# Two-layer diffusion backbone: a fifth weight buffer, a new order at the three joins, spatial mixing inside its blocks, another pace for one gate

## The chip, the cores and the metric

The kernel runs on one core of a Trainium2 chip. The metric is the device time of one execution in microseconds (us). A core has a matrix engine (TensorE, PE in the profile; PEld is its weight load), a vector engine (VectorE, DVE), a scalar engine (ScalarE, ACT), GpSimd (POOL) and SyncE (SP, which here issues DMAs). Each engine takes its instructions from its own queue in a fixed order and waits on semaphores for the others. Matrix products and transposes write to PSUM; DVE and ACT bring the results back to SBUF.

## The reference

256 latent tokens and 256 context tokens of width 2048 go through two layers. What is computed, cut to what matters here:

```python
h, hc = x, ctx
for i in range(DEPTH):                                   # layer 0: attention, layer 1: gMLP
    sh1, sc1, g1, sh2, sc2, g2 = ada_params(c[:, None, :], ada_w[i], ada_b[i])
    a = h * (1 + sc1) + sh1
    y = na_mixer(...) if i % 2 == 0 else spatial_gating_mlp(a, *gm)
    h = layer_norm(ALPHA * h + g1 * y, ln_g[i, 0], ln_b[i, 0])
    f = swiglu(h * (1 + sc2) + sh2, ffn_w_in[i], ffn_w_out[i])
    h = layer_norm(ALPHA * h + g2 * f, ln_g[i, 1], ln_b[i, 1])

def spatial_gating_mlp(a, w_in, ln_g, ln_b, w_s, b_s, w_out):
    u, v = jnp.split(jax.nn.gelu(a @ w_in, approximate=False), 2, axis=-1)
    v = layer_norm(v, ln_g, ln_b).reshape(bsz, n // CHUNK, CHUNK, N_GROUPS, GROUP_DIM)
    v = jnp.einsum("gpq,bkqgc->bkpgc", w_s, v) + jnp.transpose(b_s)[:, :, None]
    return (u * v.reshape(bsz, n, D_MODEL)) @ w_out
```

`ada_params` is a product of SiLU(c) with a 2048 by 12288 matrix per layer. Everything is float32.

## The kernel before

**Products.** Each float32 operand is split into a high part (`S.copy` to float32r, line 91) and a low part (the difference, on DVE, line 92). Every product is three matmuls, lines 86 to 88: high by high, high by low, low by high. Weights arrive in pieces of 128x1024 (512 KB): `prefetch` (line 104) issues a piece's DMA on SP into one of `RAW` = 4 raw buffers and splits it into one of five pairs of hi and lo buffers (`hiA`, `hiB`); `piece` hands out one pair and keeps four more coming. Activations are split the same way by `act_split`, into `gh` and `gl`.

**Order.** The program is written in Python order, and a scheduler turns it into one fixed queue for each engine, ahead of the run. It goes by the order in the text, `tc.high_priority(n)` lets a part count as n places earlier, and `keep_in_program_order` (`pin`) pins an instruction to its place. It works from modelled durations; on the chip the queues hold whatever the real times are.

**Side work by ticks.** The adaLN vectors are computed beside the main work. Scales and shifts are dot products on DVE (line 150), and the gates are accumulated on DVE (`gate_task`, line 174: 32 products with 512 KB each) and then summed over the partitions by one `partition_all_reduce` on POOL (`sum_task`, line 189). These tasks are paced: `tick` (line 214) is called after about every piece, adds `rate` to a credit, or 0.3 of it when it also pops a task from `side`, and runs tasks while the credit covers their cost (0.5 each here). `pace(units)` sets the rate to the cost of all tasks over `units`, so they are spread over that many ticks. `need(...)` runs what is left of a gate or shift at once.

**Attention.** Heads come one after the other; a head's scores, softmax, transposes and values are the stages in `pend`, run by `advance`. After the last head the loop at line 603 empties `pend`. The output projection (`project_out` with `w_o`) is traced behind that.

**`project_out`** (line 718) makes a 256x2048 output from `kts` blocks of 128 and writes it in two column halves `nh` of two accumulators `n` for two token halves `b` (called half 0 and half 1 below). Behind each accumulator, `residual` (line 623) takes three DVE instructions: product with the gate, ALPHA times h plus that, and `bn_stats`. For the second column half, the last `HOLD` = 4 blocks are kept back, so that half 0 can be finished while half 1's products still run.

**The joins.** `finish(b, st)` then normalises token half b and starts the next input: `Modulated.first` takes the `moments` (bn_aggr, square root on ACT, reciprocal, offset: lines 632 to 638) and for two of four column quarters q calls `part` (line 677): normalise (DVE for even q, line 646; ACT for odd q, line 682), four transposes (line 688), scale and shift by four instructions of 128x128 (lines 694 and 696), and `split_into` of the whole 128x512 quarter. The next block's held products (`block_T` with `held`) start with half 0, go on with half 1, and `rest` makes the other quarters. There are three such joins: attention's output into the FFN of layer 0 (`f0`), that FFN into the gMLP (`m1`), the gMLP's output into the FFN of layer 1 (`f1`).

**gMLP.** Four blocks make v (`gv`), each eight pieces, then four blocks make u (`gu`). The layer norm's affine part on v is a list of eight side tasks (`av`), like that of h (`a1`) before it. `spatial(nb, g2)` (line 896) mixes two groups of block nb: for each group a matmul with `ws` into PSUM (line 904) and `u = (o + bs) * u` on DVE (line 905); both groups share a PSUM bank, and the second matmul waits for the first group's DVE instruction. Then four transposes (line 909) and a copy. Block nb - 1 is mixed behind block nb; the last block's mixing goes into `side`.

Of the kernel before, what the change touches and what calls it, by code (L numbers as in the profile page):

```python
# [39 lines left out]
HK0 = 3  # L40
RAW = 4
ADA = 6
# [5 lines left out]
EARLY = tuple((3 + 4 * g + h, h, 4 * g) for g in range(3) for h in range(4))  # L48
EN = 4
EARLY_END = {HK0 + h: 12 for h in range(4)}  # L50


@with_exitstack
def hybrid_kernel(ctx: ExitStack, tc: tile.TileContext, i, out):
# [220 lines left out]
    with tc.tile_pool(name="attnX", bufs=1) as px, ExitStack() as late:  # L275
# [208 lines left out]
        def t_tile(name):  # L484
            return mp.tile([P, 512], F32, tag="t", name=name, bufs=2)

        add_tasks(0, SH2, SC2, G1)
        pace(126)
        pend = []
        with tc.tile_pool(name="attnB", bufs=1) as pb:  # L490
# [104 lines left out]
            for h in range(NH):  # L595
                if h >= HK0:
                    proj_k(h)
                proj_q(h)
                if h in V_AT_Q:
                    while len(pend) > 8:  # L600
                        advance()
                    proj_v(V_AT_Q[h])
            while pend:
                advance()

    need((0, SH2), (0, SC2))
# [37 lines left out]
    def normalise(t3, b, nb, rs):  # L644
        sl = slice(nb * 512, (nb + 1) * 512)
        V.tensor_scalar(t3[:, b, sl], t3[:, b, sl], rs[:, 0:1], rs[:, 1:2], ALU.mult, ALU.add)

# [18 lines left out]
    class Modulated:  # L666
        def __init__(self, ln, layer, tsh, tsc, name):
            self.name = name
            self.ca = main.tile([P, KT], F32, tag="ca", name=f"ca{name}", bufs=2)
            self.cb = main.tile([P, KT], F32, tag="cb", name=f"cb{name}", bufs=2)  # L670
            V.tensor_tensor(self.ca, lncol[:, ln, 0, :], cols[:, layer, tsc, :], ALU.mult)
            V.tensor_tensor(self.cb, lncol[:, ln, 1, :], cols[:, layer, tsc, :], ALU.mult)
            V.tensor_tensor(self.cb, self.cb, cols[:, layer, tsh, :], ALU.add)
            self.xh = self.xl = None
            self.rs = {}

        def part(self, b, q):
            name, ca, cb = self.name, self.ca, self.cb
            tb = slice(b * P, (b + 1) * P)
            if q % 2:  # L680
                sl = slice(q * 512, (q + 1) * 512)
                S.activation(h_t[:, b, sl], h_t[:, b, sl], AF.Identity, bias=self.rs[b][:, 1:2], scale=self.rs[b][:, 0:1])
            else:
                normalise(h_t, b, q, self.rs[b])
            ps = t_tile(f"zt{name}{b}{q}")
            for j in range(4):
                kt = 4 * q + j
                T.transpose(ps[:, j * P : (j + 1) * P], h_t[:, b, kt * P : (kt + 1) * P], ident)
            tmp = main.tile([P, 4, P], F32, tag="zt", name=f"zs{name}{b}{q}", bufs=2)
            for j in range(4):  # L690
                kt = 4 * q + j
# [3 lines left out]
                else:  # L695
                    V.tensor_scalar(tmp[:, j, :], src, ca[:, kt : kt + 1], cb[:, kt : kt + 1], ALU.mult, ALU.add)
            ks = slice(4 * q, 4 * q + 4)
            split_into(self.xh[:, ks, tb], self.xl[:, ks, tb], tmp)

        def first(self, b, st):  # L700
# [3 lines left out]
            for q in range(2):  # L704
                self.part(b, q)

        def rest(self):
# [9 lines left out]

    def project_out(kts, src, key, name, finish, extra, last=False):
        st = stats_tile(name)
        hold = LAST if last else HOLD  # L720
        for nh in range(2):
            if nh == 0:
                ps = [[acc_tile(f"po{name}{nh}{n}{b}") for b in range(2)] for n in range(2)]
# [18 lines left out]

            k0 = 0
            if nh == 1:
# [6 lines left out]
                k0 = START  # L751
            k1 = kts - hold if nh == 1 else kts
            for kt in range(k0, k1):
                if nh == 1 and kt == max(k1 - 9, k0):
                    pos["extra"] = extra()
                w = piece() if nh == 0 or kt < k1 - START else take(1)[0]
# [4 lines left out]
                if nh == 0 or kt < k1 - QUIET:  # L761
                    tick()
# [6 lines left out]
            else:  # L769
                xs, ws = fetch(k1, hold)  # L770
                for b in range(2):
                    for n in range(2):
                        for j in range(hold):
                            products(k1 + j, xs[j], ws[j], n, b)
                        with tc.high_priority(AHEAD):
                            residual(ps[n][b], b, 2 + n, g, st, name)
                    if not last:
                        with tc.high_priority(AHEAD):
                            finish(b, st)
                if last:  # L780
# [26 lines left out]

    def ffn(layer, m, key, name, finish, free, last=False):
        pg = [acc_tile(f"pg{layer}{b}") for b in range(2)]
        block_T(m, pg, True)  # L810
        free.close()
        with tc.tile_pool(name=f"ffn{layer}", bufs=1) as pf:
# [30 lines left out]

            def extra():
                return outer.tile([P, 4, 1024], F32R, tag="xT", name=f"extra{layer}")

# [8 lines left out]
        KT, lambda k: oT[:, k, :], (0, G1), "wo", m.first,  # L855
        lambda: pw.tile([P, 4, 1024], F32R, tag="w", name="extra_o"),
    )
    affine_tasks(h_t, i["ln_row"][0], "a0")
# [4 lines left out]

    def begin(b, st):
        if b == 0:
            need((1, SH1), (1, SC1), (1, SH2), (1, SC2))
            m2.append(Modulated(1, 1, SH1, SC1, "m1"))
        m2[0].first(b, st)

    ffn(0, m, (0, G2), "d0", begin, free)  # L870


    m = m2[0]
    affine_tasks(h_t, i["ln_row"][1], "a1")
    add_tasks(1, G1)
    pace(62)
    free = ExitStack()
# [17 lines left out]

    def spatial(nb, g2):
        u = us[nb]
        tp = t_tile(f"uvt{nb}{g2}")
        sp = s_tile(f"sp{nb}{g2}")
        for j in range(2):  # L900
            g = nb * 4 + g2 * 2 + j
            c = slice((g2 * 2 + j) * P, (g2 * 2 + j + 1) * P)
            o = sp[:, j * NT : (j + 1) * NT].rearrange("p (b c) -> p b c", b=2)
            T.matmul(o, ws[:, g, :], vv[:, :, g * P : (g + 1) * P], start=True, stop=True)
            V.scalar_tensor_tensor(u[:, :, c], o, bs[:, g : g + 1], u[:, :, c], ALU.add, ALU.mult)
        for j in range(2):
            c = slice((g2 * 2 + j) * P, (g2 * 2 + j + 1) * P)
            for b in range(2):
                T.transpose(tp[:, j * NT + b * P : j * NT + (b + 1) * P], u[:, b, c], ident)
        S.copy(uT[:, nb * 4 + g2 * 2 : nb * 4 + g2 * 2 + 2, :], tp)  # L910

    for nb in range(NB):
        ps = [acc_tile(f"gu{nb}{b}") for b in range(2)]
        if nb == 0:
            rs = [moments(b, st, "v")[1] for b in range(2)]
            affine_tasks(vv, i["gm_row"], "av", rs)
        block_T(m, ps, False)
        us[nb] = pg.tile([P, 2, 512], F32, tag="u", name=f"u{nb}", bufs=2)
        for b in range(2):
            S.activation(us[nb][:, b, :], ps[b], AF.Gelu)  # L920
        if nb:
            for g2 in range(2):
# [140 lines left out]
```

## Time and profile before

| what | value |
|---|---|
| median of three runs | 2418.88 us (2416.48 to 2419.06) |
| the profiled execution | 2419.84 us |
| its span, first to last instruction | 2418.1 us |
| mean granted clock of TensorE in the span | 0.996 |
| DVE / ACT / POOL busy | 73% / 46% / 5% of the span |
| HBM read over the span | 606.46 MB, 252 GB/s |

How to read it: a row of the timeline gives the start and the duration in us, the engine, the line of the code, the operation, and the output and inputs by their tile names (buffer numbers left out). In brackets stands how long the engine was idle before it and what ended that. Lines 86 to 92 belong to helpers that every stage uses, so the tile names tell the stage: `powo`, `pod` and `pogo` are output projections, `pg` and `pu` FFN blocks, `gv` and `gu` gMLP blocks, `zt` and `zs` the transposes and scaled blocks at a join, `sp` and `uvt` the spatial mixing, `lw...` the low part of a weight piece, `gl...` that of an activation block. Matmuls overlap, so a PE row of 0.39 us starts every 0.227 us.

### The profile page before, as it was taken

How to read it: one execution, taken by the hardware profiler on the slowest of the kernel's cores; microseconds unless marked ns; L12 is line 12 of the kernel's file. 1: busy time of each engine (PE TensorE's matmuls, PEld its weight loads, DVE VectorE, ACT ScalarE, POOL GpSimd, SP SyncE). 2: the span in 40 equal slices, each digit the busy share in tenths (PEclk: the TensorE clock that was granted, in tenths of full speed). 3: DMA queues.
4: the chain of work that ended last, by engine and by line, in shares of the span. 5: the costliest groups of instructions: out<-in, count | busy, mean ns of one | idle time of the engine just before them, and what ended most of it. 6: DMA issues, size and time to landing. Idle time of an engine off the chain costs nothing. (4 is left out here: it accounts for less than half of the span.)

```text
span 2418.1 us, 31362 instructions
## 1 busy us (share of the span) xinstructions
PE 2381.7 (98%) x11624; PEld 1977.0 (82%) x11624; DVE 1755.7 (73%) x2155; ACT 1122.7 (46%) x1536; POOL 109.8 (5%) x55
## 2 busy tenths in 40 slices
PE   9999999999999999999999999999999999999998
PEld 6788988888788888888888788777888888888886
DVE  4877867677788877777889788787755555576666
ACT  4344534345644444444445554446544444445553
POOL 0000000020010200000000011020100000020000
PEclk9999999999999999999999999999999999999999
DMA  9977877756679899999989677756766677656563
GB/s 382 346 265 239 272 240 238 244 164 209 197 267 338 302 334 318 320 319 320 329 287 321 202 247 270 271 177 200 235 228 228 226 233 225 207 186 195 176 212 132
DMA packets 167827, 610.64 MB, mean 253 GB/s; under 512 B 19349, under 2 KB 21717, under 8 KB 163317
## 3 DMA queue, kind: packets, MB, share of 16 engines
q1 hardware_dynamic: 121172, 440.74, 54.3%
q10 hardware_dynamic: 46372, 167.86, 20.1%
q8 instruction: 91, 1.49, 0.3%
q14 instruction: 64, 0.52, 0.1%
q0 software_dynamic: 128, 0.03, 0.0%
HBM read 606.46 MB, written 2.10 MB: 252 GB/s over the span
## 5 line engine op out<-in xcount | busy, mean ns | idle before, releaser
L92 DVE TENSOR_TENSOR lwf<-rwf,hwf 128x1024 fp32r<-128x1024 f32 x320 | 407.2, 1275 | 278.9 <-ACT hwf L91 278.6
L91 ACT CAST hwf<-rwf 128x1024 fp32r<-128x1024 f32 x320 | 337.1, 1054 | 490.5 <-PE pu L88 221.6
L86 PE MATMUL pod<-hwd,ghd 128*128 128x512 f32 x684 | 266.4, 390 | 0.0
L87 PE MATMUL pod<-lwd,ghd 128*128 128x512 f32 x684 | 266.2, 389 | 0.0
L88 PE MATMUL pod<-hwd,gld 128*128 128x512 f32 x684 | 265.8, 389 | 0.0
L92 DVE TENSOR_TENSOR lwd<-rwd,hwd 128x1024 fp32r<-128x1024 f32 x172 | 212.2, 1235 | 64.0 <-ACT hwd L91 63.8
L150 DVE SCALAR_TENSOR_TENSOR ad<-ad,c_bc 128x1024 f32<-128x1024 f32 x192 | 232.6, 1219 | 0.6 <-DMA ad<-in_ada_t 0.6
L91 ACT CAST hwd<-rwd 128x1024 fp32r<-128x1024 f32 x172 | 180.6, 1050 | 54.8 <-PE pod L88 28.8
L174 DVE SCALAR_TENSOR_TENSOR gate<-ag,c_col,gate 128x1024 f32<-128x1024 f32 x128 | 163.2, 1282 | 0.0
L88 PEld LDWEIGHTS pod<-hwd,gld 128*128 128x128 f32 x684 | 128.3, 188 | 26.8
L86 PEld LDWEIGHTS pod<-hwd,ghd 128*128 128x128 f32 x684 | 128.4, 188 | 26.7 <-DVE sg L838 0.3
L87 PEld LDWEIGHTS pod<-lwd,ghd 128*128 128x128 f32 x684 | 128.4, 188 | 26.6
L86 PE MATMUL pg<-hwf,f1h 128*128 128x512 f32 x320 | 126.4, 395 | 0.0
L86 PE MATMUL pg<-hwf,f0h 128*128 128x512 f32 x320 | 126.4, 395 | 0.0
L87 PE MATMUL pg<-lwf,f0h 128*128 128x512 f32 x320 | 124.6, 389 | 0.4 <-DVE lwf L92 0.4
L88 PE MATMUL pg<-hwf,f1l 128*128 128x512 f32 x320 | 124.7, 390 | 0.0
L88 PE MATMUL pg<-hwf,f0l 128*128 128x512 f32 x320 | 124.7, 390 | 0.0
L86 PE MATMUL pu<-hwf,f0h 128*128 128x512 f32 x320 | 124.5, 389 | 0.0
L87 PE MATMUL pu<-lwf,f0h 128*128 128x512 f32 x320 | 124.5, 389 | 0.0
L88 PE MATMUL pu<-hwf,f0l 128*128 128x512 f32 x320 | 124.5, 389 | 0.0
L86 PE MATMUL pu<-hwf,f1h 128*128 128x512 f32 x320 | 124.5, 389 | 0.0
L87 PE MATMUL pu<-lwf,f1h 128*128 128x512 f32 x320 | 124.5, 389 | 0.0
(343 smaller groups left out, 5338.5 us busy)
## 6 DMA issues: line engine op xcount, KB each, us to landing
rwf<-in_w_in_t SPq DMA_DIRECT2D x320, 512.0 KB
ad<-in_ada_t ACTq DMA_DIRECT2D x192, 512.0 KB
rwd<-in_w_out SPq DMA_DIRECT2D x176, 512.0 KB
ag<-in_ada_g ACTq DMA_DIRECT2D x128, 512.0 KB
rwg<-in_w_gin SPq DMA_DIRECT2D x64, 512.0 KB
ap<-in_ada_p SPq DMA_DIRECT2D x20, 1024.0 KB
rwq<-in_w_q SPq DMA_DIRECT2D x32, 512.0 KB
rwo<-in_w_o SPq DMA_DIRECT2D x32, 512.0 KB
```

Of the source, the lines that this page charges most:

```text
L86: keep(T.matmul(ps, sh, mh, start=first, stop=False))
L87: keep(T.matmul(ps, sh, ml, start=False, stop=False))
L88: keep(T.matmul(ps, sl, mh, start=False, stop=last))
L91: S.copy(hi, src)
L92: V.tensor_tensor(lo, src, hi.bitcast(F32), ALU.subtract)
L150: pin(V.scalar_tensor_tensor(r, r, 1.0, c_bc[:, half * 1024 : (half + 1) * 1024], ALU.mult, ALU.mult, accum_out=o[:, nt : nt + 1],))
L174: pin(V.scalar_tensor_tensor(g, loaded.pop(key), c_col[:, kt, 0:1], g, ALU.mult, ALU.add))
```

## The change

It does seven things. There are five raw weight buffers in place of four. The first steps of attention's output projection are traced inside the loop that empties `pend`: two behind the last head's scores, one behind its transposes (`out_begin`, `WHILE`). At a join, half 1's residuals are queued behind half 0's first normalisation on DVE (`issue_after`). In `part`, for q = 0, the split is made two blocks at a time. The scales of the second join (`Modulated` m1) are made earlier, with the extra buffer. The gate of layer 1's mixer is paced over 44 units in place of 62. And `spatial` is cut into four steps, two `mix` and two `turn`, that `block_T` runs behind the third to sixth piece of the next block (the last block's four go into `side`).

```diff
-RAW = 4
+RAW = 5
+WHILE = {3: 2, 1: 1}
+        def out_begin(kts, src, name):
+            ps = [[acc_tile(f"po{name}0{n}{b}") for b in range(2)] for n in range(2)]
+
+            def step(kt):
+                w = piece()
+                x = act_split(src(kt), f"{name}0_{kt}")
+                for n in range(2):
+                    c = slice(n * 512, (n + 1) * 512)
+                    for b in range(2):
+                        tb = slice(b * P, (b + 1) * P)
+                        mm3(ps[n][b], x[0][:, tb], x[1][:, tb], w[0][:, c], w[1][:, c], kt == 0, kt == kts - 1)
+                tick()
+
+            return ps, step
...
+            wo_ps, wo_step = out_begin(KT, lambda k: oT[:, k, :], "wo")
+            wo_k = 0
             while pend:
                 advance()
+                for _ in range(WHILE.get(len(pend), 0)):
+                    wo_step(wo_k)
+                    wo_k += 1
...
-                normalise(h_t, b, q, self.rs[b])
+                ins = normalise(h_t, b, q, self.rs[b])
+                self.mark = self.mark or ins.ins
...
+            cut = 2 if q == 0 else 4
...
-            ks = slice(4 * q, 4 * q + 4)
-            split_into(self.xh[:, ks, tb], self.xl[:, ks, tb], tmp)
+                if (j + 1) % cut == 0:
+                    ks = slice(kt + 1 - cut, kt + 1)
+                    split_into(self.xh[:, ks, tb], self.xl[:, ks, tb], tmp[:, j + 1 - cut : j + 1, :])
...
+                m = None
                 for b in range(2):
                     for n in range(2):
                         for j in range(hold):
                             products(k1 + j, xs[j], ws[j], n, b)
-                        with tc.high_priority(AHEAD):
+                        with tc.high_priority(AHEAD), tc.issue_after(m.mark) if m else nullcontext():
                             residual(ps[n][b], b, 2 + n, g, st, name)
                     if not last:
                         with tc.high_priority(AHEAD):
-                            finish(b, st)
+                            m = finish(b, st)
...
-    def begin(b, st):
-        if b == 0:
-            need((1, SH1), (1, SC1), (1, SH2), (1, SC2))
-            m2.append(Modulated(1, 1, SH1, SC1, "m1"))
-        m2[0].first(b, st)
+    def prepare():
+        need((1, SH1), (1, SC1), (1, SH2), (1, SC2))
+        m2.append(Modulated(1, 1, SH1, SC1, "m1"))
...
-    pace(62)
+    pace(44)
...
+        def mix(g2):
+            sp = s_tile(f"sp{nb}{g2}")
+            for j in range(2):
...
+                T.matmul(o, ws[:, g, :], vv[:, :, g * P : (g + 1) * P], start=True, stop=True)
+                V.scalar_tensor_tensor(u[:, :, c], o, bs[:, g : g + 1], u[:, :, c], ALU.add, ALU.mult)
+
+        def turn(g2):
+            tp = t_tile(f"uvt{nb}{g2}")
...
+            S.copy(uT[:, nb * 4 + g2 * 2 : nb * 4 + g2 * 2 + 2, :], tp)
+
+        return [partial(f, g2) for f in (mix, turn) for g2 in range(2)]
...
-        block_T(m, ps, False)
+        block_T(m, ps, False, spatial(nb - 1) if nb else ())
...
-        if nb:
-            for g2 in range(2):
-                spatial(nb - 1, g2)
-    side.extend((lambda: spatial(NB - 1, 0), lambda: spatial(NB - 1, 1)))
+    side.extend(spatial(NB - 1))
```

More of the change, by code (lines that the diff above doesn't have):

```diff
@@ L1 @@
-from contextlib import ExitStack
+from contextlib import ExitStack, nullcontext
 from functools import partial
@@ L645, in normalise @@
         sl = slice(nb * 512, (nb + 1) * 512)
-        V.tensor_scalar(t3[:, b, sl], t3[:, b, sl], rs[:, 0:1], rs[:, 1:2], ALU.mult, ALU.add)
+        return V.tensor_scalar(t3[:, b, sl], t3[:, b, sl], rs[:, 0:1], rs[:, 1:2], ALU.mult, ALU.add)
     def affine_tasks(t3, src, name, rs=None):
@@ L675, in __init__ @@
             self.rs = {}
+            self.mark = None
         def part(self, b, q):
@@ L705, in first @@
                 self.part(b, q)
+            return self
         def rest(self):
@@ L716, in hybrid_kernel, with project_out @@
     AHEAD = 400
-    def project_out(kts, src, key, name, finish, extra, last=False):
+    def project_out(kts, src, key, name, finish, extra, last=False, begun=None):
         st = stats_tile(name)
@@ L722, in project_out @@
             if nh == 0:
-                ps = [[acc_tile(f"po{name}{nh}{n}{b}") for b in range(2)] for n in range(2)]
+                ps, step, k0 = begun or (*out_begin(kts, src, name), 0)
+                for kt in range(k0, kts):
+                    step(kt)
             else:
@@ L741, in fetch @@
                 return xs, take(n)
-            k0 = 0
             if nh == 1:
@@ L751, in project_out @@
                 k0 = START
-            k1 = kts - hold if nh == 1 else kts
-            for kt in range(k0, k1):
-                if nh == 1 and kt == max(k1 - 9, k0):
+            k1 = kts - hold
+            for kt in range(k0, k1) if nh == 1 else ():
+                if kt == max(k1 - 9, k0):
                     pos["extra"] = extra()
-                w = piece() if nh == 0 or kt < k1 - START else take(1)[0]
+                w = piece() if kt < k1 - START else take(1)[0]
                 x = act_split(src(kt), f"{name}{nh}_{kt}")
@@ L760, in project_out @@
                         products(kt, x, w, n, b)
-                if nh == 0 or kt < k1 - QUIET:
+                if kt < k1 - QUIET:
                     tick()
@@ L806, in block_T, with ffn @@
                 turn.pop(0)()
-    def ffn(layer, m, key, name, finish, free, last=False):
+    def ffn(layer, m, key, name, finish, free, last=False, prepare=None):
         pg = [acc_tile(f"pg{layer}{b}") for b in range(2)]
@@ L844, in extra @@
             def extra():
+                if prepare:
+                    prepare()
                 return outer.tile([P, 4, 1024], F32R, tag="xT", name=f"extra{layer}")
@@ L856, in hybrid_kernel @@
         lambda: pw.tile([P, 4, 1024], F32R, tag="w", name="extra_o"),
+        begun=(wo_ps, wo_step, wo_k),
     )
@@ L862, in hybrid_kernel @@
     m2 = []
-    def begin(b, st):
-        if b == 0:
-            need((1, SH1), (1, SC1), (1, SH2), (1, SC2))
-            m2.append(Modulated(1, 1, SH1, SC1, "m1"))
-        m2[0].first(b, st)
-    ffn(0, m, (0, G2), "d0", begin, free)
+    def prepare():
+        need((1, SH1), (1, SC1), (1, SH2), (1, SC2))
+        m2.append(Modulated(1, 1, SH1, SC1, "m1"))
+    ffn(0, m, (0, G2), "d0", lambda b, st: m2[0].first(b, st), free, prepare=prepare)
     m = m2[0]
@@ L894, in hybrid_kernel, with spatial @@
     us = {}
-    def spatial(nb, g2):
+    def spatial(nb):
         u = us[nb]
[L898 to L910, printed above, removed]
+        def mix(g2):
+            sp = s_tile(f"sp{nb}{g2}")
+            for j in range(2):
+                g = nb * 4 + g2 * 2 + j
+                c = slice((g2 * 2 + j) * P, (g2 * 2 + j + 1) * P)
+                o = sp[:, j * NT : (j + 1) * NT].rearrange("p (b c) -> p b c", b=2)
+                T.matmul(o, ws[:, g, :], vv[:, :, g * P : (g + 1) * P], start=True, stop=True)
+                V.scalar_tensor_tensor(u[:, :, c], o, bs[:, g : g + 1], u[:, :, c], ALU.add, ALU.mult)
+        def turn(g2):
+            tp = t_tile(f"uvt{nb}{g2}")
+            for j in range(2):
+                c = slice((g2 * 2 + j) * P, (g2 * 2 + j + 1) * P)
+                for b in range(2):
+                    T.transpose(tp[:, j * NT + b * P : j * NT + (b + 1) * P], u[:, b, c], ident)
+            S.copy(uT[:, nb * 4 + g2 * 2 : nb * 4 + g2 * 2 + 2, :], tp)
+        return [partial(f, g2) for f in (mix, turn) for g2 in range(2)]
     for nb in range(NB):
```

## The prediction

> **What bounds the kernel now.** First the page's head, to see which engine fills the span. Then the waits of PE (total us, times, longest).
>
> ```profile
> span 2418.1 us, 31362 instructions
> PE 2381.7 (98%) x11624; PEld 1977.0 (82%) x11624; DVE 1755.7 (73%) x2155; ACT 1122.7 (46%) x1536; POOL 109.8 (5%) x55
> ...
> PE pt L575 <- ACT p L565: 3.7, 2, 3.4
> PE ztf L688 <- ACT zsf L694: 2.3, 2, 1.2
> PE pogo L88 <- DVE glgo L92: 2.3, 2, 1.3
> PE sp L904 <- DVE u L905: 2.1, 1, 2.1
> ...
> PE pg L86 <- ACT f0h L91: 1.8, 2, 1.6
> PE pg L86 <- ACT f1h L91: 1.8, 2, 1.6
> PE gv L86 <- ACT m1h L91: 1.8, 2, 1.6
> ...
> PE s L86 <- ACT qh L515: 0.3, 1, 0.3
> ```
>
> TensorE is busy for 98%, and the change leaves all its products in place. So only its waits can be won: one inside attention (pt), two at each of the three joins (pg or gv, then zt), one in the first spatial mix (sp), two in the gMLP output (pogo). A wait costs more than its length where the clock drops. The windows view shows it (PE busy, clock, DMA share):
>
> ```profile
> 642.20:645.60 3.40, 1.62 (x7) 1.00 0.46 145
> 645.60:649.00 3.40, 3.40 (x9) 0.50 0.17 57
> 1382.87:1386.28 3.41, 2.10 (x8) 1.00 0.49 159
> 1522.80:1526.20 3.40, 3.34 (x11) 0.50 0.79 321
> 1673.00:1676.40 3.40, 3.40 (x10) 0.50 0.29 82
> ```
>
> Three stretches of 3.4 us ran at half clock, each behind a wait, and cost 1.7 us each. At the second join PE was busy for 2.10 of 3.41 us and the clock held; at the first, for 1.62 of 3.40, and it fell.
>
> The Trainium skill ("TensorE: Matmul & The Clock Gate", Part 1) throttles after a whole idle window of about 3.4 us. Here 1.8 idle us in 3.4 sufficed, so the rows decide; by the page alone the joins would have no half clock to lose, and the sum below would be 3.4 us higher.
>
> **The joins.** DVE and then ACT at the second join, from the timeline:
>
> ```profile
> 1378.70 0.67 DVE L626 TENSOR_TENSOR yd<-pod,gate 128x512 f32<-128x512 f32 x1
> 1379.29 0.15 DVE L638 SCALAR_TENSOR_TENSOR rsm<-mvm,rsm 128x1 f32<-128x1 f32 x1
> 1379.40 0.69 DVE L627 SCALAR_TENSOR_TENSOR h_t<-h_t,yd 128x512 f32<-128x512 f32 x1
> 1380.01 0.54 DVE L646 TENSOR_SCALAR h_t<-h_t,rsm 128x512 f32<-128x512 f32 x1
> ...
> 1379.26 1.06 ACT L91 CAST hwg<-rwg 128x1024 fp32r<-128x1024 f32 x1 [0.67 <-PE pod L88]
> 1380.21 1.52 ACT L682 ACTIVATE h_t<-h_t,rsm 128x512 f32<-128x512 f32 x2
> 1381.64 1.83 ACT L694 ACTIVATE zsm<-ztm,cbm,cam 128x128 f32<-128x128 f32 x5
> 1383.35 0.62 ACT L91 CAST m1h<-zsm 128x512 fp32r<-128x512 f32 x1
> ```
>
> Half 1's product (L626) and sum (L627) stand on either side of L638, which yields half 0's offset, and ahead of half 0's normalisation (L646). Issued behind it, they free 1.1 us on DVE (L646 from 1380.01 to about 1378.95). ACT's cast of the next weights at 1379.26 stays, so ACT's own normalisation (L682) doesn't move; the casts by twos do the rest. m1h waited for five L694 at 0.34 us; now it waits for two and casts half the columns: 1.0 us for the three, and 0.2 us for the cast (an estimate: the 128x256 casts of gh take 0.41 us). That is 1.2 us at least, 2.3 if all of DVE's lead counts, against 1.8 waited. I take 1.6 each, **-4.8** for three; the rest stays as a wait for m1l, which still queues on DVE behind a 1.2 us weight difference. The waits for zs at the transposes of half 1 fall by the same casts: **-1.5** of 2.8 (2.3 at the FFN joins, 0.5 at the second). Half clocks at two joins: **-3.4**.
>
> What is late next is half 1. Its chain starts at the end of PE's products, which hardly moves, while PE now comes 1.6 to 3.3 us sooner to its transposes:
>
> ```profile
> 1387.53 1.22 DVE L92 TENSOR_TENSOR extra<-rwg,extra 128x1024 fp32r<-128x1024 f32 x1
> 1388.66 0.54 DVE L646 TENSOR_SCALAR h_t<-h_t,rsm 128x512 f32<-128x512 f32 x1
> ...
> 650.21 1.00 DVE L646 TENSOR_SCALAR h_t<-h_t,rsf 128x512 f32<-128x512 f32 x2
> ...
> 652.08 1.03 PE L688 MATMUL ztf<-ident,h_t 128*128 128x128 f32 x8
> ```
>
> At the second join the last normalisation ends at 1389.20 and PE wanted it at 1389.36: no slack. At the first the earlier of two normalisations ended at 650.75 (0.54 behind 650.21), and PE came at 652.08: 1.3 us to spare. So new waits of about 0.9 us at the second join and 1.4 at each FFN join: **+3.7** (bounds 0, if the weight differences leave the chain, and 6). The joins together: **-6.0**, from -10 to 0. Half 1's first residual, queued behind the normalisation, is itself 0.5 us later; the second can't start before PE's last products, so nobody waits for that. Moving the column scales (`prepare`) ahead takes three DVE instructions of 0.16 us out of a place that isn't on this path: 0.
>
> **The sum of the gate, moved by pace 44.** The (1, G1) gate is 32 products at 0.5 and one partition sum at 0.5: 16.5 units. gv has 28 ticks and gu 32, of which the 16 with a side task count 0.3. At 62 the 32nd product fell into the gMLP output. At 44 it needs 16/0.375 = 42.7 counted ticks: after tick 36 there are 24.8, so tick 54, the second piece of gu's last block. The count can be checked: at 62 the 23rd product (11.5/0.266 = 43.2) belongs to tick 55, the third piece of that block, and there it is:
>
> ```profile
> 1557.30 1.23 DVE L92 TENSOR_TENSOR lwg<-rwg,hwg 128x1024 fp32r<-128x1024 f32 x1 [1.50 <-ACT hwg L91]
> 1558.44 1.28 DVE L174 SCALAR_TENSOR_TENSOR gate<-ag,c_col,gate 128x1024 f32<-128x1024 f32 x1
> ...
> 1558.24 0.39 PE L87 MATMUL gu<-lwg,m1h 128*128 128x512 f32 x1
> 1558.47 0.39 PE L88 MATMUL gu<-hwg,m1l 128*128 128x512 f32 x1
> ...
> 1605.01 12.78 POOL L189 PARTITION_ALL_REDUCE gate<-gate  x1 [101.88 <-DVE gate L174]
> 1606.02 9.30 DVE L92 TENSOR_TENSOR glgo<-uT,ghgo 128x256 fp32r<-128x256 f32 x1
> ...
> 530.59 8.84 DVE L92 TENSOR_TENSOR lwq<-rwq,hwq 128x1024 fp32r<-128x1024 f32 x1
> ```
>
> The partition sum on POOL starts right behind the last product, and the next difference of two SBUF operands on DVE, 0.42 us long elsewhere, hangs until 10.3 us after its start. Both big waits that aren't joins come from this: pt (530.59) and pogo (1606.02). At its new place the last product runs one piece (twelve matmuls 0.227 us apart, 2.72 us) before 1558.44, ends near 1557.0, and DVE is shut until 1567.3. The change puts the mixes of spatial(2) behind the third and fourth piece of that block, at 1558.5 and 1561.2, and each mix needs DVE between its two matmuls:
>
> ```profile
> 1522.33 0.87 DVE L905 SCALAR_TENSOR_TENSOR u<-sp,bs,u 128x256 f32<-128x256 f32 x2
> 1512.31 6.50 DMA rwg<-in_w_gin
> ```
>
> (There sp waited 2.1 us for L905 alone.) PE takes its queue in order, so everything behind the second matmul waits. If the weight difference of 1557.30, 0.3 us after the sum's start, still slips through, the first mix passes and the second holds PE from 1562 to 1568, 6.2 us; if not, the first does, from 1559.2 to 1568, 8.8 us. I take **+6.5**, nearer to the first, and one stretch of half clock, **+1.7**. In exchange the pogo waits go: **-2.3**.
>
> The Trainium skill ("SBUF — State Buffer", Who interferes with whom) has a DVE instruction with at most one SBUF input free of GpSimd. L905 reads PSUM and one SBUF tile, so by the page it would pass; but it queues behind differences with two.
>
> **The first mix, and the fifth buffer.** spatial(0) moves from behind its block into it, behind the third piece. That hides the mix under products, but nearer to the eight `av` tasks, which keep DVE full (the second row is DVE's alone: 29.3 of 30 us):
>
> ```profile
> 1450.00:1470.00 20.00, 20.00 (x90) 16.57 (x89) 17.19 (x16) 9.30 (x10) 0.00 (x0) 1.00 1.00 361
> ...
> 1480.00:1510.00 30.00, 29.30 (x36) 1.00 0.60 202
> ...
> 1505.46 0.39 PE L88 MATMUL gu<-hwg,m1l 128*128 128x512 f32 x1
> 1509.93 1.22 DVE L92 TENSOR_TENSOR lwg<-rwg,hwg 128x1024 fp32r<-128x1024 f32 x1
> ```
>
> PE ends the third piece at 1505.7; DVE is through with what comes ahead of the mix at about 1511. Some of these 5.5 us are in the planned order, so I take a wait of 1.6 us with its half clock, 3.3, against 2.1 + 1.7 now: **-0.5** (from -3.8 to +6.0, rival 3). The fifth raw buffer lets the piece issued at 1512.31 (6.50 us to land) start one release earlier. No PE wait but this one follows such a landing, so I give it 0 by itself (from -1 to 0.5, the length of the smaller waits); its 4 KB a partition take no engine's time. The gate's loads come denser too: 512 KB of weights and 0.75 of 512 KB in a tick of 2.72 us make 337 GB/s. From 1450 to 1470 DMA moved 361 GB/s, and PE was busy for all 20 us: hidden.
>
> **Attention's tail.** The three steps of the output projection ahead of the last transposes fill a place in which PE lists only the 0.3 us of s: the scheduler already puts this projection's products there. The pt wait lies a head earlier and stays. **-0.3** (0 to -0.8).
>
> **The sum**, against the profiled execution's own 2419.84 us (span 2418.1 and 1.7 around it): -6.0 - 2.3 + 6.5 + 1.7 - 0.5 - 0.3 = -0.9, so 2418.9. That run lies 0.96 above the median of the three, 2418.88; so **2418.0 us**, no change that can be measured. About 0.2%, 4.8 us, is what a measurement of this kernel can tell.
>
> **The rivals.**
> 1. *The sum misses the mixes.* If the last product runs two pieces earlier or later than counted, as products in pogo ran ahead of their ticks, DVE is shut between mixes. For it: DVE has no other reason to hold L174 back. Against it: four products of the last two gu blocks stand at the counted piece. +8.2 becomes about +0.5: **2410.3**. Chance 0.28.
> 2. *Half 1 isn't late.* If its normalisations move ahead of the weight differences, the 3.7 us go: **2414.3**. Nothing in the order of before says so. 0.10.
> 3. *Slower.* The gates come 1.4 times as often, so by the first mix DVE has done six products more; two of them (2.6 us) fall in the full stretch. Then L905 comes 8.1 us after PE asks, with 1.7 of half clock: 9.8 against 3.8 now, 6.5 more than taken: **2424.5**. It decides once DVE is over 7 us behind at the third piece of gu's second block. 0.20.
>
> **How the numbers follow.** The forecast has 0.42, with 2412 to 2424 as its own range (joins from -10 to 0, the hold from 6.2 to 8.8). Of it I count 0.07 as faster and 0.06 as slower; rival 1 gives 0.27, rival 2 0.06, rival 3 0.16. So faster 0.40, same 0.38, slower 0.22. The range that leaves 2 in 10 out is **2406 to 2426**.
>
> **What would show it.** A POOL sum starting near the second piece of gu's last block, a DVE difference of 9 us behind it, and a PE wait of 6 to 9 us on sp show the main step right; sums elsewhere, or mixes through before it, show it wrong. At the joins L646 should stand right behind L638, m1h should be cast in 128x256 pieces, and the first pg and gv waits be under 0.6 us; a longer wait of zt for L646 or L682 shows half 1 late. Half-clock stretches: one in gu's last block, none at the joins.

## The result, and the profile after

| | us | against before |
|---|---|---|
| before, median of 5 runs | 2418.88 (2416.48 to 2421.66) | |
| changed kernel, median of 5 runs | 2429.06 (2427.12 to 2429.58) | 1.0042, 95% interval 1.0027 to 1.0057 |
| its profiled execution | 2429.58, span 2427.5 | 9.74 above the profiled execution of before |

The change made the kernel slower by 0.42%, 10.2 us; 2418.0 was forecast. In the rows of the changed kernel L93 is the difference of a split (before: L92), L175 the gate's product (L174), L647 to L649 the residual (L626 to L628), L667 the normalisation on DVE (L646), L711 the transposes (L688), L934 and L935 the two halves of a spatial mix (L904, L905; L906 and L907 in the kernels that are the one before with the twos).

The page's head:

```profile
span 2427.5 us, 31382 instructions
PE 2381.7 (98%) x11624; PEld 1978.0 (81%) x11624; DVE 1757.8 (72%) x2161; ACT 1121.8 (46%) x1542; POOL 106.6 (4%) x55
```

PE is busy for the same 2381.7 us as before, so the loss is waiting and slowed products. PE's waits (total, times, longest):

```profile
PE sp L934 <- DVE u L935: 10.9, 2, 7.8
PE ztf L711 <- DVE h_t L667: 3.6, 4, 1.5
PE pt L591 <- ACT p L581: 3.4, 1, 3.4
...
PE ztm L711 <- DVE h_t L667: 1.8, 2, 1.5
...
PE gv L87 <- ACT m1h L92: 1.1, 1, 1.1
PE gv L89 <- DVE m1l L93: 0.9, 1, 0.9
```

The rows of pg for f0 and f1 are those of gv for m1 within 0.1. The wait for sp was 2.1 us and is 10.9. The transposes now wait for L667 some 1.8 us at each join, 1.5 of it (the longest) for half 1, where before they waited 0.2 for half 0 alone. The wait for a first cast is 1.1, not 1.6; the 1.1 is half 1's, though (the timeline has it behind half 1's transposes). The pogo waits (2.3) are gone. The stretches of half clock, each under the stretch ahead of it (PE busy, clock, DMA share, GB/s), from the windows view:

```profile
647.77:651.18 3.41, 1.71 (x11) 1.00 0.84 268
651.18:654.59 3.41, 3.41 (x10) 0.50 0.25 103
1385.05:1388.46 3.41, 1.61 (x11) 1.00 0.84 258
1388.46:1395.29 6.83, 5.99 (x17) 0.50 0.28 101
1511.30:1514.70 3.40, 0.68 (x3) 1.00 0.89 307
1514.75:1518.16 3.41, 3.41 (x9) 0.50 1.00 382
1562.53:1565.95 3.42, 0.04 (x1) 1.00 0.00 0
1565.95:1576.19 10.24, 5.82 (x14) 0.50 0.33 104
```

Two lie at joins, one behind spatial(0), one in gu's last block. Half of PE's busy time in them is lost: 1.7, 3.0, 1.7 and 2.9 us. (Attention's tail has a stretch of its own in every trace here, 3.41 us long in some and 6.83 in others, with the change or without, and so has the end.) What happened in that last block, from the timeline:

```profile
1558.34 1.28 DVE L175 SCALAR_TENSOR_TENSOR gate<-ag,c_col,gate 128x1024 f32<-128x1024 f32 x1
...
1559.72 11.88 POOL L190 PARTITION_ALL_REDUCE gate<-gate  x1 [54.63 <-DVE gate L175]
1559.83 10.09 DVE L93 TENSOR_TENSOR lwg<-rwg,hwg 128x1024 fp32r<-128x1024 f32 x1 [0.21 <-ACT hwg L92]
...
1561.27 0.60 PE L934 MATMUL sp<-vv,ws 128*128 128x256 f32 x2
...
1569.84 0.47 DVE L935 SCALAR_TENSOR_TENSOR u<-sp,bs,u 128x256 f32<-128x256 f32 x1
...
1570.37 1.22 PE L934 MATMUL sp<-vv,ws 128*128 128x256 f32 x2 [7.80 <-DVE u L935]
```

The last product of the gate ends, the partition sum starts, and the weight difference 0.11 us behind it takes 10.09 us. The first mix of spatial(2) begins on PE 1.55 us behind the sum's start; its part on DVE runs only at 1569.84, behind that difference, and PE's next product of the mix waited 7.80 us for it.

By stage, from the first and last products of each (the profiled executions, in order): start -2.8 us, attention's tail +0.2, first join -1.1, second join with gv +4.9, gu +15.1, gMLP output -5.9, third join with the last FFN -0.9. The start's -2.8 isn't the change's: its first query product comes at 153.4 to 154.1 in all the runs below, with four raw buffers too, and only the one profiled execution of before has 156.2. Some 2.6 us of gu's +15.1 and the output's -5.9 are spatial(2) itself, which moved from the one stage to the other.

### The profile page after: what moved, and what is told of

The parts are those of the page before. It is cut to its first block, busy times and chain, and to the rows that moved or that the text cites. A ratio compares the mean times of both kernels' runs of the same rounds, so it can differ in the third digit from the quotient of the medians.

```text
span 2427.5 us, 31382 instructions
## 1 busy us (share of the span) xinstructions
PE 2381.7 (98%) x11624; PEld 1978.0 (81%) x11624; DVE 1757.8 (72%) x2161; ACT 1121.8 (46%) x1542; POOL 106.6 (4%) x55
## 4 chain that ended last, share of the span: by engine, by line
PE 93%; DVE 4%; DMA 1%; issue 1%; ACT 1%; POOL 0%; DVEq 0%; SPq 0%; POOLq 0%; ACTq 0%
PE pu L87 7%; PE pu L88 7%; PE pu L89 7%; PE pod L88 6%; PE pod L89 6%; PE pod L87 6%; PE pg L87 6%; PE pg L89 6%; PE pg L88 6%; PE vps L87 2%; PE vps L88 2%; PE vps L89 2%; PE kps L88 2%; PE kps L89 2%; PE kps L87 2%; PE qps L89 1%
## 5 line engine op out<-in xcount | busy, mean ns | idle before, releaser
L93 DVE TENSOR_TENSOR lwf<-rwf,hwf 128x1024 fp32r<-128x1024 f32 x320 | 406.1, 1272 | 275.8 <-ACT hwf L92 275.8
L92 ACT CAST hwf<-rwf 128x1024 fp32r<-128x1024 f32 x320 | 336.8, 1053 | 484.2 <-PE pu L89 242.2
L93 DVE TENSOR_TENSOR lwd<-rwd,hwd 128x1024 fp32r<-128x1024 f32 x172 | 210.0, 1223 | 63.0 <-ACT hwd L92 62.7
L92 ACT CAST hwd<-rwd 128x1024 fp32r<-128x1024 f32 x172 | 180.3, 1048 | 55.3 <-PE pod L89 33.3
L175 DVE SCALAR_TENSOR_TENSOR gate<-ag,c_col,gate 128x1024 f32<-128x1024 f32 x128 | 163.7, 1286 | 0.0
L89 PE MATMUL pu<-hwf,f1l 128*128 128x512 f32 x320 | 124.5, 389 | 0.0
```

The source lines that it names most:

```text
L89: keep(T.matmul(ps, sl, mh, start=False, stop=last))
L92: S.copy(hi, src)
L93: V.tensor_tensor(lo, src, hi.bitcast(F32), ALU.subtract)
L175: pin(V.scalar_tensor_tensor(g, loaded.pop(key), c_col[:, kt, 0:1], g, ALU.mult, ALU.add))
```

## The experiments

Theory: the sum of the gate under the mixes of spatial(2) made the loss. Rivals: the joins made it; or the sum costs the same wherever it stands. Each ratio is to runs of before on the same chip (their medians were 2415.9 to 2417.6), with its 95% interval; 0.1% is 2.4 us.

| | what it is | ratio |
|---|---|---|
| e1 | changed kernel, pace 62 | 1.0026 (1.0015 to 1.0037) |
| e2 | changed kernel, pace 39.5 | 1.0021 (1.0012 to 1.0029) |
| e3 | changed kernel, no tie | 1.0023 (1.0014 to 1.0031) |
| e4 | changed kernel, no twos | 1.0051 (1.0038 to 1.0065) |
| e5 | no tie, pace 39.5, mixes two pieces later | 1.0006 (0.9997 to 1.0015) |
| e6 | no tie, pace 39.5 | 0.9987 (0.9978 to 0.9996) |
| e7 | before with the twos | 0.9983 (0.9974 to 0.9992) |
| e8 | before with the fifth buffer | 0.9982 (0.9973 to 0.9990) |
| e9 | before with twos and fifth buffer | 0.9970 (0.9958 to 0.9982) |
| e10 | e9 at pace 39.5 | 1.0019 (1.0010 to 1.0028) |
| e11 | no tie, pace 39.5, mixes behind blocks | 1.0018 (1.0009 to 1.0027) |
| e12 | changed kernel, mixes behind blocks | 0.9999 (0.9990 to 1.0008) |
| e13 | e9 at pace 44 | 0.9983 (0.9974 to 0.9992) |
| e14 | no tie, pace 62 | 1.0000 (0.9991 to 1.0010) |

### Where the sum stands (e1, e2, e12)

```diff
-    pace(44)
+    pace(62)      # e1
+    pace(39.5)    # e2
```

> The changed kernel, but the gate's products are spread at pace 62 as before the change, so that its partition sum goes back into the gMLP output. Theory A (the loss is the sum standing under the mixes of spatial(2)): the 7.98 us wait of sp and the half clock behind it go, some 11 us, and the pogo wait with its half clock comes back, some 4 us: about 2422 us (2419 to 2425), so no longer slower than before by more than 0.2%. Rival B (the loss comes from the joins, whose new waits and half clocks stay here): within 3 us of the changed kernel's 2429. Rival C (the sum costs the same wherever it stands): 2427 to 2430, with a PE wait of about 8 us in the gMLP output.

> The changed kernel with pace 39.5: by the count of ticks the 32nd product then belongs to the sixth piece of gu's third block, and the sum's 10 us of DVE lie between the mixes of spatial(1) and those of spatial(2). Theory A: the partition sum starts near that piece, one DVE difference behind it still takes 9 to 10 us, but PE waits for none of it: no sp wait over 2 us in the last block, no pogo wait: 2418 us (2415 to 2421), some 11 us under the changed kernel. Rival C (wherever the sum stands in gu, PE runs out of weights while DVE is shut): a PE wait of 5 us or more behind the long difference and 2424 or more. Rival B (the joins): 2427 to 2430.

Both came out in between: 0.16% and 0.21% below the changed kernel, not 0.3 to 0.45%. The 7.8 us wait went in both, as the theory had it. In e1 its place was taken by a wait in the gMLP output (PE's waits):

```profile
PE pogo L89 <- DVE glgo L93: 4.3, 2, 3.3
...
PE sp L934 <- DVE u L935: 2.8, 1, 2.8
```

142 of the output's products start ahead of the sum here, and 118 before: it came two pieces of twelve products later. (By the clock it stands 34.9 us behind the output's first product here, 1609.93 less 1575.05, and 32.0 before, 1605.01 less 1572.98; the 2.6 us of spatial(2) lay in that stretch before.) By the code, this is because the changed kernel's spatial(3) is cut into four side parts, not two, each of whose ticks counts 0.3. DVE's backlog then ran into the residual of the output's first half: in e14, which has the same two pogo waits, L647 to L649 fill DVE from 1624.00 to 1629.97, ahead of the split that PE wanted at 1627. In e2 the denser gates made the first mix worse:

```profile
PE sp L934 <- DVE u L935: 5.2, 2, 4.8
```

So the wait that the theory named went, and other costs came in its place; these two runs alone don't say what the sum's place is worth. e12 leaves the sum where the change puts it and takes the mixes away from it:

```diff
-        return [partial(f, g2) for f in (mix, turn) for g2 in range(2)]
+        return [partial(f, g2) for g2 in range(2) for f in (mix, turn)]
...
-        block_T(m, ps, False, spatial(nb - 1) if nb else ())
+        block_T(m, ps, False)
...
+        if nb:
+            for part in spatial(nb - 1):
+                part()
```

> The changed kernel with only the spatial mixes taken back behind their blocks: tie, twos, pace 44 and fifth buffer stay. Theory: the sum still starts at the second piece of gu's last block (about 1558 us) and one difference on DVE still takes 10 us, but spatial(2) comes behind the block, when DVE is free again, so the 8 us wait and its half clock (11 us) go, and the wait of spatial(0) falls from 3.4 to 1 to 2.5 us: 10 to 14 us less than the changed kernel, 2415 to 2419, within 0.2% of before. Rival: PE runs out of weights during the 10 us (a wait on lwg of 5 us or more in the last block), and the time stays over 2424.

It is 0.43%, 10.4 us, below the changed kernel, as expected. The sum still starts there, 3.3 us earlier by the clock, and DVE (timeline) still stands still:

```profile
1555.08 1.28 DVE L175 SCALAR_TENSOR_TENSOR gate<-ag,c_col,gate 128x1024 f32<-128x1024 f32 x1
1556.65 11.14 DVE L93 TENSOR_TENSOR lwg<-rwg,hwg 128x1024 fp32r<-128x1024 f32 x2 [0.30 <-ACT hwg L92]
1567.72 3.48 DVE L93 TENSOR_TENSOR lwgo<-rwgo,hwgo 128x1024 fp32r<-128x1024 f32 x3
...
1572.74 0.92 DVE L935 SCALAR_TENSOR_TENSOR u<-sp,bs,u 128x256 f32<-128x256 f32 x2
```

Two differences take 11.14 us where such a one takes 1.22 elsewhere, yet PE (windows: PE busy, clock, DMA share, GB/s) goes on:

```profile
1540.00:1590.00 50.00, 49.39 (x227) 1.00 0.49 162
```

The weights cast ahead carry PE through 10 us without DVE. What can't be carried is a mix, which needs DVE between two matmuls. That settles the theory against both rivals for this term: same joins, same pace, the same sum in the same block, and the 10 us are gone.

### The tie of half 1's residual, and the twos (e3, e4, e6, e7)

```diff
-                        with tc.high_priority(AHEAD), tc.issue_after(m.mark) if m else nullcontext():
+                        with tc.high_priority(AHEAD):      # e3
...
-            cut = 2 if q == 0 else 4
+            cut = 4                                        # e4
```

> The changed kernel, but the residual of half 1 isn't tied behind the normalisation of half 0 (only that tie is taken out; the casts by twos stay). The tie took the 0.67 and 0.69 us of half 1 out of half 0's way at three joins. If it is worth what the prediction gave it (two thirds of 1.6 us a join), the first PE waits (gv and pg for m1h, f0h, f1h) grow by about 1 us each and half 1's waits at the transposes (1.70 and 1.35) shrink by as much or less: 2429 to 2432. If half 1 is what decides the joins now, the first waits grow and half 1's shrink by the same, and the time stays within 1.5 us of 2429.

> The changed kernel, but the first blocks are cast whole again (four transposed blocks at a time). Half 0's first cast then comes some 1 us later at each join. If half 0 decides: the first waits for m1h, f0h and f1h go from 1.1 to about 2 us and half 1's waits fall: 2429 to 2432. If half 1 decides (PE comes too soon to its transposes in any case): within 1.5 us of 2429, or up to 3 us below it, since the three small casts and three differences that the twos add go off ACT and DVE ahead of half 1's normalisation.

Neither expectation for e3 was right: without the tie the kernel is 0.19% faster. The same pair at the other paces gives 0.34% (e2 less e6) and 0.26% (e1 less e14): some 5 to 8 us. e3's waits at the joins:

```profile
PE gv L87 <- ACT m1h L92: 1.3, 2, 0.6
...
PE gv L89 <- DVE m1l L93: 0.7, 1, 0.7
...
PE ztm L711 <- DVE h_t L667: 0.2, 1, 0.2
```

(pg's for f0 and f1 are the same within 0.1.) About 2.2 us a join, against 3.8 with the tie (1.8, 1.1 and 0.9). The tie does save half 0's first product its wait of 0.6; but half 1 pays 1.5 for L667 and 0.5 more for its own cast. DVE at the second join shows how. With the tie (changed kernel), from half 1's second residual to its normalisation:

```profile
1378.98 0.69 DVE L647 TENSOR_TENSOR yd<-pod,gate 128x512 f32<-128x512 f32 x1
...
1380.53 1.22 DVE L93 TENSOR_TENSOR lwg<-rwg,hwg 128x1024 fp32r<-128x1024 f32 x1
1381.66 0.68 DVE L649 BATCH_NORM_STATS2 std<-h_t 128x6 f32<-128x512 f32 x1
...
1382.86 0.25 DVE L653 BATCH_NORM_AGGREGATE mvm<-std 128x2 f32<-128x24 f32 x1
...
1385.37 1.22 DVE L93 TENSOR_TENSOR lwg<-rwg,hwg 128x1024 fp32r<-128x1024 f32 x1
1386.50 1.00 DVE L667 TENSOR_SCALAR h_t<-h_t,rsm 128x512 f32<-128x512 f32 x2
```

Without it (e3):

```profile
1376.50 1.21 DVE L93 TENSOR_TENSOR lwg<-rwg,hwg 128x1024 fp32r<-128x1024 f32 x1
...
1377.94 0.68 DVE L647 TENSOR_TENSOR yd<-pod,gate 128x512 f32<-128x512 f32 x1
...
1379.85 0.69 DVE L649 BATCH_NORM_STATS2 std<-h_t 128x6 f32<-128x512 f32 x1
...
1380.90 0.26 DVE L653 BATCH_NORM_AGGREGATE mvm<-std 128x2 f32<-128x24 f32 x1
...
1384.16 1.00 DVE L667 TENSOR_SCALAR h_t<-h_t,rsm 128x512 f32<-128x512 f32 x2
1385.08 1.22 DVE L93 TENSOR_TENSOR lwg<-rwg,hwg 128x1024 fp32r<-128x1024 f32 x1
```

L667 stands 7.52 us behind the second L647 with the tie and 6.22 without. The second residual starts at PE's last product either way. But half 1's first residual, put behind half 0's normalisation, takes the place in which DVE did a weight difference (1376.50); with the tie that difference falls into half 1's chain, ahead of L649, and another goes ahead of L667.

No trace of a kernel with the twos and without the tie has a half clock at a join (e3, e5, e6, e7, e9, e10, e11, e13, e14); each trace with the tie has at least one (changed kernel, e1, e2, e4, e12).

e4, the tie without the twos, is 0.09% above the changed kernel, inside what the runs can tell. Its waits for L667 are 5.3 us at the three joins as with the twos (5.4), its zs waits are back (3.8), and its waits for first casts are shorter (1.7 for 3.3): nearer to the second answer. The twos by themselves:

> The kernel before with the first blocks cast by twos, nothing else of the change. The prediction's -4.8 for the first waits came from DVE's order and the twos together. If the twos do it alone: the waits of 1.6 us for f0h, f1h and m1h fall to about 0.6 each, the zs waits go, and one or two half clocks with them: 4 to 6 us below before. If the tie is needed for it: first waits of 1.2 or more, and within 2 us of before.

0.17%, 4.1 us. The waits of e7 at the second join, and below them that of before for the low part:

```profile
PE gv L86 <- ACT m1h L91: 1.3, 2, 0.6
...
PE gv L88 <- DVE m1l L92: 0.7, 1, 0.7
```

```profile
PE gv L88 <- DVE m1l L92: 0.2, 1, 0.2
```

At each join the waits for a cast went from 1.8 to 1.3 (two of 0.6), but the wait for the low part rose by as much. What the twos won are the zs waits (2.8 us at the three joins) and the half clocks there; e7's 11 runs have a mean granted clock of 0.9968 and the 33 of before on that chip 0.9959, which puts some 2 us of the gain down to the clock. The tie isn't needed for it.

> The changed kernel without the tie and at pace 39.5; mixes where the change puts them. If the two gains are separate (tie some 5 us, sum some 8 us on the same chip), this is the changed kernel less 12 to 13 us: 2415 to 2418, within 0.2% of before, with an sp wait of 3 to 5 us left at spatial(0) and no other wait over 2 us behind the second join. If they overlap (half clocks shared), 2419 to 2421.

0.13% below before, 2415.8 us where before is 2418.9: the gains of pace and tie add up.

### The mixes inside the blocks (e5, e10, e11, e14), and the best version (e8, e9, e13)

```diff
-    def block_T(m, ps, held, turn=()):
+    def block_T(m, ps, held, turn=(), at=2):
...
-            if turn and k2 >= 2:
+            if turn and k2 >= at:
...
+        block_T(m, ps, False, spatial(nb - 1) if nb else (), 4)
```

> The changed kernel without the tie of half 1's residual, at pace 39.5, and with the four parts of a spatial mix behind the fifth to eighth piece of a block in place of the third to sixth. Theory: the first mix of spatial(0) waits because DVE is still behind with the av rows and the gate's products when PE asks behind the third piece; two pieces (5.4 us) later DVE has caught up. Then the sp waits (5.2 us at pace 39.5) fall under 1.5 us, the half clock of gu's second block goes, and with the tie gone the joins' 1.5 us waits of half 1 too: 0.2 to 0.5% below before, 2407 to 2414 us. Rival: DVE stays behind by as much (it is full as long as gates come at this pace), the wait is 4 us again two pieces later, and the time is that of e6.

The theory failed: two pieces later costs 0.19% against e6, and the first mix still waits 3.9 us, as the rival had it (not the rival's time). PE came to the first mix at 1508.91, and DVE had this ahead of it (timeline):

```profile
1511.37 1.28 DVE L175 SCALAR_TENSOR_TENSOR gate<-ag,c_col,gate 128x1024 f32<-128x1024 f32 x1
1512.57 1.22 DVE L93 TENSOR_TENSOR lwg<-rwg,hwg 128x1024 fp32r<-128x1024 f32 x1
1513.70 1.28 DVE L175 SCALAR_TENSOR_TENSOR gate<-ag,c_col,gate 128x1024 f32<-128x1024 f32 x1
1514.90 1.22 DVE L93 TENSOR_TENSOR lwg<-rwg,hwg 128x1024 fp32r<-128x1024 f32 x1
1516.03 0.47 DVE L935 SCALAR_TENSOR_TENSOR u<-sp,bs,u 128x256 f32<-128x256 f32 x1
...
1545.56 9.31 DVE L93 TENSOR_TENSOR lwg<-rwg,hwg 128x1024 fp32r<-128x1024 f32 x1 [0.16 <-ACT hwg L92]
1554.80 0.47 DVE L935 SCALAR_TENSOR_TENSOR u<-sp,bs,u 128x256 f32<-128x256 f32 x1
```

DVE hadn't caught up: it had a difference and a product to do for each piece. And the last two lines show the sum reaching the mixes of spatial(1), which now stood later (the row of 1554.80 is one of theirs; PE's transposes behind it waited 3.7 us). e10 and e11 show the same from the other side, with the mixes behind the blocks at pace 39.5.

> As the run with twos and the fifth buffer, and the gate's products at pace 39.5 in place of 62, with the spatial mixes behind their blocks as before. The sum then stands in gu's third block. If the mix only waits because it was moved into the block: no sp wait over 2.5 us here, the pogo waits (1.9 to 2.8 us) gone, 2 to 4 us less than at pace 62. If the denser gates leave DVE behind also at the block's end: sp wait of 3 us or more with its half clock, and no less than at pace 62.

> The changed kernel without the tie, at pace 39.5, and with the spatial mixes behind their blocks as before; what is left of the change is the twos, the fifth buffer, the projection's steps in attention's tail and the earlier column scales. Against the same with mixes inside the blocks (0.13% below before, sp wait of 4.5 us and 6.8 us of half clock): if moving the mixes into the block is itself a loss, 4 to 7 us less than that, 0.3 to 0.4% below before; if the gates' density alone makes the wait, the same 0.1% below before. Against the run with twos, fifth buffer and pace 39.5 it shows what attention's tail is worth: the prediction gave 0.3 us, so the same within a microsecond.

Both were 0.18% to 0.19% above before, and e11 missed both of its answers. The sum at 39.5 starts at 1541.28 in e10, and gu's third block ends at 1545.8, where spatial(1) follows (PE's waits of e10):

```profile
PE sp L906 <- DVE u L907: 9.6, 2, 6.2
```

The 6.2 is the changed kernel's collision at another place. The other 3.5 us are the first mix, which waits with its half clock also behind its block: the second answer for e10. At 39.5 the mixes inside the blocks are clear of the sum (e6) and those behind them aren't, at 44 the other way round. e11 equals e10 within 0.13%, so the projection's steps in attention's tail and the earlier scales are worth nothing that these runs show. With the sum out of reach of both, at pace 62:

> The changed kernel without the tie and at pace 62; the mixes stay inside their blocks. Against the run with twos and fifth buffer alone (0.30% below before) this differs in the mixes' place (and the projection's steps in attention's tail, worth nothing so far). If the place is itself a loss at this pace: sp wait of 2 to 3 us with a half clock in gu's second block, pogo waits of 3 to 4 us, 2415 to 2420 us on the scale where before is 2418.9. If the place costs only with dense gates or under the sum: 2410 to 2413.

It equals before, and is 0.30%, 7.3 us, above e9. The first answer holds: sp waits 3.1 us and pogo 4.3, each with a half clock. So moving the mixes loses also without the sum beside them: at the first mix directly, and in the output, where the sum comes two pieces later as in e1.

> The kernel before with five raw weight buffers, nothing else. The changed kernel came 2.8 us earlier out of the start stage (first qps product 153.38 for 156.15) with the same instructions there; the runs tell whether the fifth buffer does that. If it does: 153 to 154 and 2 to 3 us below before. If not (the start's waits for ap differ from run to run): 156 and within 1 us of before, as the prediction had it.

The start's gain isn't the buffer's (e7 with four buffers has 153.75 too), and yet the buffer alone is worth 0.18%, 4.4 us. At the first mix, before (from the prediction) L905 came at 1522.33, 3.04 us behind PE's first sp matmul at 1519.29. With five buffers (timeline, PE and DVE) it came 1.61 us behind:

```profile
1514.65 1.03 PE L904 MATMUL sp<-vv,ws 128*128 128x256 f32 x4
...
1516.26 0.87 DVE L905 SCALAR_TENSOR_TENSOR u<-sp,bs,u 128x256 f32<-128x256 f32 x2
```

The wait fell from 2.1 to 0.7, with no half clock behind it. In the last 10 us ahead of that mix DVE stood idle for a cast of weights for 0.67 and 1.02 us before, and for 0.39 here, which fits pieces that arrive earlier. The half clock of the first join went too, with that join's waits unchanged. But single traces overstate what the clock gave: e8's 11 runs have a mean granted clock of 0.9962, the 33 of before on that chip 0.9959, under 1 us. The waits that went (sp 1.4, pogo 0.4) make 1.8 us; where the rest of the 4.4 lies stays open.

> The kernel before with the casts by twos and the fifth raw buffer, nothing else of the change. Alone they came out 0.17% and 0.18% below before. If they win different waits (the twos those of the first products and zs at the joins, the buffer that of sp): 0.3 to 0.4% below before, 2409 to 2412 us where before is 2418.9, with no sp wait over 1 us and first waits under 0.8. If both won the same half clocks: 0.2% below.

> The kernel before with the casts by twos, the fifth raw buffer and pace 44; mixes behind their blocks. The sum then starts in gu's last block near 1550 us and its 10 us of DVE end before spatial(2). If the pogo waits (1.9 us at pace 62) were the sum's price there, they go; in exchange sp waits at spatial(0) as in the run with mixes behind at pace 44 (2.6 us for 0.9). So within 2 us of the run at pace 62, 0.25 to 0.4% below before: the placing of the sum, clear of the mixes, is worth little either way. If DVE's longer shut time starves PE: an lwg wait of over 2 us in the last block, and 0.2% below before or less.

e9 is the best of all: 2409.37 us beside 2417.09 for before on that chip, 0.30% (0.18 to 0.42%) below before and, by the two ratios, 0.7% below the changed kernel. Its one half clock ahead of the last store is in attention's tail; none is left at a join or in gu. e13, the sum in gu's last block, clear of the mixes, came 0.13% above it, with about 0.15% of uncertainty, and short of the 0.25% expected: its pogo waits went, but sp waited 2.7 us for 0.9, with a half clock. PE didn't run out of weights in that block.

## Why the prediction was wrong, step by step

From the runs the change adds up so: twos and buffer -0.30%, mixes inside the blocks +0.30% (e14 less e9), pace 44 +0.23% (e3 less e14), tie +0.19% (changed kernel less e3): +0.42%. Each is a step from one of these kernels to the next, so they must add up; each has about 0.15% of uncertainty, and another order would give other shares (at pace 39.5 the mixes inside the blocks win 0.31%, e6 less e11). The step of the mixes also holds attention's tail and the earlier scales.

- **The joins, -6.0: the step that failed.** Measured by stage they gave +2.9 (-1.1, +4.9 with gv, -0.9). By terms, over the three joins: the first waits, -4.8, gave -0.2 (casts 3.3 us for 5.4, low parts 2.5 for 0.6); the zs waits, -1.5, gave -2.8; half 1, +3.7, cost +5.0 (L667 is waited for 5.4 us for 0.4); the half clocks, -3.4, came to +1.3.
  - The tie was taken for a gain. "Half 1's first residual, queued behind the normalisation, is itself 0.5 us later; the second can't start before PE's last products, so nobody waits for that" is the sentence that fell. The second residual did start on time; what follows it didn't, since a weight difference was pushed behind it. The prediction saw half 1 late but blamed PE's earlier arrival; e3, e6 and e14 show the tie to be the cause: without it, the wait for L667 is 0.2 us a join. So rival 2, half 1 not late, is what the kernels without the tie show.
  - The 1.6 us taken off each first wait came in no run, with the tie or without. Half 0's first cast does come sooner, but PE then waits for the low part and for half 1's cast.
  - That the joins without the tie win nearly what was forecast (-5.0 by stage in e7) is luck: it comes from the zs waits and the half clocks alone.
- **The half clocks at joins, -3.4:** +1.3. The stretches there cost 1.7 and 3.0 where they cost 3.4 before, as the new waits of half 1 left PE busy for 1.71 and 1.61 us of 3.41, close to the 1.62 that had lost the clock before.
- **The sum under the mixes, +6.5 and +1.7:** mechanism and place were right: the first mix came 1.55 us behind the sum's start, where 1557.0 and 1558.5 had been said. The size was off. Of the two answers, that the weight difference still slips through and that it doesn't, I took a value near the first; it didn't, so the first mix was held, for 7.8 us, and half clock lasted three times as long as the one stretch that I had counted, and cost 2.9 us: 10.7 for 8.2. What held the mix was the difference queued ahead of it, not its own instruction: e5 has an L935 at 1544.92, 0.24 us behind the start of its sum (1544.68), and it took its usual 0.48 us. e12's -10.4 holds this and the first mix's share.
- **pogo, -2.3:** they went.
- **The first mix, -0.5:** the sp wait was 3.1 with a half clock of 1.7, so +1.0 against before: between the 1.6 that I took and the 8.1 of rival 3. But rival 3's mechanism, DVE behind with the gate's products, is what e2, e5 and e13 show.
- **The fifth buffer, 0:** in the kernel before it is worth -4.4 by itself, outside the -1 to 0.5 that I gave it. I had seen that the one wait it can touch is sp's, and then not taken that wait out. That wait, with its half clock, is part of the 4.4; the rest is open.
- **Attention's tail, -0.3:** nothing that the runs can tell (e11 and e10).

Rival 1, the sum missing the mixes, wasn't what happened; e12 makes it so, and the gain was 10.4 us where the rival counted 7.7.

## What to carry to other kernels

An instruction tied behind another doesn't only move itself: ask which instruction takes the place that it leaves, and whether that one then stands in the next chain. A task that shuts an engine for 10 us is free where PE has its operands ahead, and costs most of its length (7.8 of 10.1 us here) where PE hands that engine something and waits for it back; so fix its place relative to such hand-overs, and recount it whenever either moves. And try the plain parts of a change alone: two small ones were worth 0.30% here, and the other three took all of it back and more.

## What the hardware showed that was not expected

- With the wait of 7.8 us came 10.24 us of half clock, three times the 3.41 us of most stretches. It began inside the wait, at 1565.95, and ran on 5.8 us past its end at 1570.37.
- The same waits don't always cost the clock: e8 has the join waits of before (1.8 us for each first cast) and ran the first join at full clock, where before had 3.4 us of half clock. The Trainium skill ("TensorE: Matmul & The Clock Gate", Part 1) describes a free-running window of about 3.4 us. The traces agree: behind the start stage, the half-clock stretches of a trace all begin whole numbers of 3.413 us apart. Those of the changed kernel begin at 538.54, 651.18, 1388.46, 1514.75 and 1565.95, which are 33, 216, 37 and 15 windows apart. Counted in these windows, the wait for the first join's first cast fell into one before (PE busy for 1.63 us of it), and across two in e8 (2.45 and 2.53). Over all the traces, a full-clock window with 1.52 us or less of PE busy was always followed by half clock, one with 1.87 or more never, and from 1.56 to 1.82 both occurred. No run here placed a wait on purpose.
- The partition sum took 11.88 us in gu and 12.78 us in the gMLP output, on the same tile (the profile's spans on POOL are rough).
